# HGRN score steps in smaller pieces, and the sums for a fast matrix product issued in another place and rank

## The chip, the cores and the metric

The kernel runs on one core of a Trainium2 chip. The metric is the device time of one execution in microseconds (us); the median of three runs is 1410.47 us (1410.33 to 1411.88).

## The reference, cut to what matters

One transformer-like block over 256 tokens of width 2048. A normalised input goes through one combined projection; an HGRN2 branch and a chunked attention branch are gated and merged, projected, and followed by a squared-ReLU MLP.

```python
u = rms_norm(h, norm_mix_w)
hq, hf, hi, hg, aq, ak, av, gates = jnp.split(u @ w_in, SPLIT_POINTS, axis=-1)
g = lb + (1.0 - lb) * sigmoid(hf);  log_g = log(g);  kk = 1.0 - g
q = silu(hq) * HG_DK ** -0.5
# per chunk of 64 tokens, 8 heads of 128 channels: b = cumsum(log_g)
scores = einsum('bhtk,bhtsk,bhsk->bhts', qc, exp(b_t - b_s) where t >= s, kc)
o = scores @ v + (decayed state) ...
y_a = rms_norm(o, hg_norm_w) * silu(hg);  y_b = chunk_band_attention(aq, ak, av, rel_bias)
h = h + (gate_a * (y_a @ w_branch_a) + gate_b * (y_b @ w_branch_b)) @ w_out
h = h + square(relu(rms_norm(h, norm_mlp_w) @ w_up)) @ w_down
out = rms_norm(h, norm_final_w)
```

All is float32. w_in has 11,264 columns, w_up and w_down 8192 columns and rows.

## The kernel before, in words

**Matrix products.** Every float32 matrix is split into a high part (a cast on ScalarE, ACT, line 89) and a low part (a subtraction on VectorE, DVE, line 90), and each product is three matmuls on TensorE (PE): high by high, high by low, low by high (lines 143 to 145; 184, 185 and 188 for the transposed form). Weights come in pieces over the SyncE DMA queue into rings of buffers (`raw`, `wh`, `wl`); `split` and the copies and subtractions that TensorE waits for are written inside `tc.high_priority(offset=2000)`.

**Order on the engines.** The kernel is written for a planner: each engine's queue is laid out beforehand, by an operation's rank (its place in the program's text, moved up by 2000 under `high_priority`) among those whose operands and buffers are expected to be ready. On the chip each engine then keeps its queue's order and waits on semaphores. `tc.issue_after(ins)` adds an order edge: what is written in its block stays behind `ins` on the engine of `ins`, with no semaphore.

**HGRN.** The eight heads are done in four pairs (`fq(0)` to `fq(3)`); pairs 0 and 1 make group 0, pairs 2 and 3 group 1. For a pair, `hf_pair` makes the decay g, the keys `kk` and the running sum `b` (a Sigmoid, a logarithm, a scan), `hq_pair` the queries `q` (a Sigmoid). `hgrn_scores` makes the scores of a pair with small matmuls at four levels: `diagonal` (line 372), three `level`s with block sizes 2, 8 and 32 (line 416), and `level128` (line 448). Each level multiplies left factors `kl` by right factors `qr` that `factors` makes on DVE and ACT with exponentials (lines 383 to 405), and merges the product, by mask, from PSUM into `sd` (line 423; `diagonal` at 373 and 374). `hgrn_out` multiplies the scores by `v` (lines 476, 477), normalises and gates into `o` (line 487), and `finish` transposes it (line 494). PSUM for these small products is a ring of two banks (`ps_sm`).

The small steps are spread between the k-tiles of the large projections: `later(...)` appends pairs of a gap in ticks and a step to the list `behind`, and each k-tile of a projection calls `tick`, which counts the gap of the first one down (two ticks for a k-tile in `gemm`, one in `gemm_t`) and runs it at zero. The projections follow in the order hf, hq of pairs 0 and 1, hi of group 0, hg of group 0, hf and hq of pair 2, hf and hq of pair 3, hi and hg of group 1, then the first two of aq.

**Units.** The larger products after that (half of the gates, w_out, w_up, w_down) go through `Unit` and `run`. A unit covers 1024 output columns; for the first half of its rows it uses seven block products instead of eight, which needs sums of weight blocks (`sums` on DVE, `sent` by an accumulating DMA on GpSimd's queue) and sums of blocks of the left operand (`combos`: `one`, `two` and two more `final`s, lines 640 to 657, with a split for each sum into tiles `S`). Partial products go from one PSUM bank to another through `copy` (ACT, line 756) and `less` (DVE, line 783). The second half of the rows is done plainly, in `plain` items of two k-tiles; the last two items of a unit are run within the next unit.

A unit also carries `steps`: transposes of blocks of the next left operand (`one`) and the sums (`combos`). At eleven places of `run`, numbered 0 to 10, `step(at)` runs the first step in the list if `at` has reached the step's own third entry or the unit's `start`. `plain` first runs every step whose first entry is not above its rows' block number (2 or 3): these are forced. The places, in order: ahead of product 12, ahead of product 11 (second), ahead of item (8, 9), ahead of product 21 (first), [first copy `u1`], ahead of item (10, 11), [`less` of 12], ahead of product 21 (second), [second copy `u2`], 6: ahead of item (8, 9) of the other columns, [`less` of 22], 7, 8, 9 and 10 ahead of the remaining item, the last product and the last two items. The steps concerned: `h_blocks(0)` in unit `wo2` (sums of h for w_up), and `turns(0)` in units `up02`, `up12`, `up22` and `up32` (sums of u, the squared-ReLU output, for w_down).

Of the kernel before, what the change touches and what calls it, by code (L numbers as in the profile page):

```python
# [50 lines left out]
def tile_hybrid_block(  # L51
# [107 lines left out]
    def later(*steps):  # L159
        behind.extend([n, f] for n, f in steps)  # L160
# [149 lines left out]
    def hf_pair(u, f):  # L310

        nc.vector.tensor_tensor(f, f, bc(rstd_t, 1, 2), op=ALU.mult)
        nc.scalar.activation(f, f, AF.Sigmoid)
        for h in range(2):
            hh = 2 * u + h
            nc.vector.tensor_scalar(f[:, h, :], f[:, h, :], omlb[:, hh:hh + 1], lb[:, hh:hh + 1],
                                    op0=ALU.mult, op1=ALU.add)
        kk = h2(f"kk{u}")
        nc.vector.tensor_scalar(kk, f, -1.0, 1.0, op0=ALU.mult, op1=ALU.add)
        nc.vector.tensor_scalar(f, f, LN_MIN, None, op0=ALU.max)  # L320
        lg = h2(f"lg{u}")
        nc.scalar.activation(lg, f, AF.Ln)
        b = h2(f"b{u}")
        nc.vector.tensor_tensor_scan(b.rearrange("p h t -> p (h t)"), reset,
                                     lg.rearrange("p h t -> p (h t)"), 0.0, ALU.mult, ALU.add)
        return f, kk, b
# [32 lines left out]
            gws.append(s)  # L359
        return gws  # L360

    def hgrn_scores(n, kk, b, q):
# [92 lines left out]
        def both(*fs):  # L455
            def go():
                for x in fs:
                    x()
            return go

        return (sd, so), [both(diagonal, f[0]), both(l[0], f[1]), both(l[1], f[2]), both(l[2], factors128), level128]

    ya = []

# [46 lines left out]

    def scores(n, a, gap, first=None):
        sc, steps = hgrn_scores(n, *a)
        later(*[(gap if i or first is None else first, f) for i, f in enumerate(steps)])
        return sc

    def group(g, s0, s1, vs, gws, gap, gap2):
        o0, f0 = hgrn_out(g, 0, s0, vs, gws)
        o1, f1 = hgrn_out(g, 2, s1, vs, gws)
        later(*[(gap, f) for f in o0 + o1], *[(gap2, f) for f in f0 + f1])  # L520
# [209 lines left out]
    class Unit:  # L730
# [22 lines left out]

        def copy(self, dst, i):
            with tc.high_priority(offset=2000):
                nc.scalar.copy(dst, self.c[i])
            return dst

        def product(self, i, name, left, first=False):
# [20 lines left out]

        def less(self, i, t):
            with tc.high_priority(offset=2000):
                nc.vector.tensor_tensor(self.c[i], self.c[i], t, op=ALU.subtract)

        def sums(self, dst, src):
            with tc.high_priority(offset=2000):
# [185 lines left out]
    def h_blocks(n0):  # L972

        def one(n, m):
            if not m:
                hT.append(new_act(f"h{n}"))
            hi, lo = hT[n][:, :, 0, :], hT[n][:, :, 1, :]
            t = h1[n][m]
            tp = transpose4(t, f"h{n}{m}")
            tmp = fours(token(f"hw_{n}_{m}"))  # L980
            nc.vector.tensor_tensor(tmp, tp, bc(wmlp[:, 4 * n:4 * n + 4], 2, P), op=ALU.mult)
            split(hi[:, :, m * P:(m + 1) * P], lo[:, :, m * P:(m + 1) * P], tmp)
            nc.scalar.activation(token(f"hsq_{n}_{m}"), t, AF.Square, accum_out=ssq2[:, m, n:n + 1])

        def factor():
            ssum2 = small.tile([P, NM], F32, name="ssum2", tag="ssum")
            nc.vector.tensor_reduce(ssum2, ssq2, axis=AX.X, op=ALU.add)
            rsqrt(rstd2, ssum2, D, NM)

        return [(n, lambda n=n, m=m: one(n, m)) for n in (n0, n0 + 1) for m in range(NM)] + [  # L990
            (n0 + 1, f, 7) for f in ([factor] if n0 else combos(hT, "h", sp, Sh))]

    rstd2 = const.tile([P, NM], F32, name="rstd2")

    def h_out(m, n, acc):
        t = token(f"h1_{n}_{m}")
        with tc.high_priority(offset=2000):
# [7 lines left out]
    rstd3 = const.tile([P, NM], F32, name="rstd3")  # L1005
    NQ = 4
    units = [Unit(lambda: mT, lambda: Sm, w_out, n0 * NC, f"wo{n0}", lambda m, n, acc, n0=n0: h_out(m, n0 + n, acc),
                  steps=(lambda: h_blocks(0)) if n0 else (lambda: turned(mT, 3, "m3", ga)), start=3 if n0 else 0) for n0 in (0, 2)]
    fin = {}
    for qd in range(NQ):  # L1010
        last = qd == NQ - 1
# [2 lines left out]
        def turns(c0, uT=uT, rs=rs, Su=Su, blocks=blocks, qd=qd):  # L1014

            def one(c, m):
                if not m:
                    uT.append(new_act(f"u{qd}{c}"))
                hi, lo = uT[c][:, :, 0, :], uT[c][:, :, 1, :]
                tp = transpose4(rs[c, m], f"u{qd}{c}{m}")  # L1020
                if c < 2:
                    blocks[m, c] = fours(token(f"a{m}{c}_u{qd}"))
                    nc.scalar.copy(blocks[m, c], tp)
                split(hi[:, :, m * P:(m + 1) * P], lo[:, :, m * P:(m + 1) * P], tp)

            return [(c, lambda c=c, m=m: one(c, m)) for c in (c0, c0 + 1) for m in range(NM)] + [
                (c0 + 1, f, 7) for f in ([] if c0 else combos(uT, f"u{qd}", tk, Su, blocks))]

        for c in range(0, 4, 2):
            def done(m, n, acc, c=c, rs=rs, qd=qd):  # L1030
                t = token(f"r{qd}{c}{n}{m}")
                with tc.high_priority(offset=2000):
                    nc.scalar.activation(t, acc, AF.Relu, scale=rstd2[:, m:m + 1])
                nc.scalar.activation(t, t, AF.Square)
                rs[c + n, m] = t

            units.append(Unit(lambda: hT, lambda: Sh, w_up, qd * (FF // NQ) + c * NC, f"up{qd}{c}", done,
                              steps=(lambda turns=turns: turns(0)) if c else (lambda: ()) if qd else (lambda: h_blocks(2)), start=3 if c else 0))

        def out_of(m, n, acc, last=last, qd=qd):  # L1040
            if not last:
# [85 lines left out]
```

## Time and profile before

| | us |
|---|---|
| median of three runs | 1410.47 (1410.33 to 1411.88) |
| the profiled execution | 1411.28 |
| its span, first to last instruction | 1409.5 |
| PE busy | 1387.3 |
| DVE busy | 1119.1 |
| ACT busy | 909.0 |
| GpSimd busy | 137.0 |

In a line of the profile stand the engine, the source line (L416), the tile written and the tiles read. "<-" before an engine and a tile names what ended the idle time in front of an instruction. PEclk is the TensorE clock that was granted, as a share of full speed. A matmul's own duration overlaps with its neighbours'; the distance between starts is what one costs.

### The profile page before, as it was taken

What the parts mean: (1) busy time and instruction counts of PE and PEld (TensorE: products, weight loads), DVE (VectorE), ACT (ScalarE), POOL (GpSimd) and SP (SyncE); (2) the same over time, 40 slices, a digit from 0 to 9 for tenths busy, and PEclk for the clock granted to TensorE, in tenths of its full rate; (3) what the DMA queues carried; (4) which work ended last, traced back from release to release, by engine and by line L of the source; (5) the groups of instructions that cost most, each with busy time, mean ns of one, the idle gap of its engine ahead of it and who ended that gap; (6) DMA issues with size and microseconds to landing.
All of it is one profiled execution on the core that took longest, in us unless ns stands there. A gap on an engine that the chain in (4) does not pass through costs nothing.

```text
span 1409.5 us, 18582 instructions
## 1 busy us (share of the span) xinstructions
PE 1387.3 (98%) x6562; PEld 1149.8 (82%) x6562; DVE 1119.1 (79%) x1410; ACT 909.0 (64%) x1170; POOL 137.0 (10%) x220
## 2 busy tenths in 40 slices
PE   9999999999999999999999999999999999999997
PEld 7878888878787888888778888888888888888885
DVE  7897987675657875687999878789777897878885
ACT  6755745464556665445767876677666876668764
POOL 2000001010000000001210001100111001110200
PEclk9999999999999999999999999999999999999999
DMA  9644445665568987558898898998899888998883
GB/s 336 219 156 156 144 157 162 191 172 167 177 224 262 259 236 257 188 176 254 245 292 263 242 277 225 288 279 249 258 290 292 249 229 252 286 298 261 259 247 118
DMA packets 122925, 327.42 MB, mean 232 GB/s; under 512 B 10944, under 2 KB 11712, under 8 KB 122448
## 3 DMA queue, kind: packets, MB, share of 16 engines
q1 hardware_dynamic: 103264, 264.80, 54.8%
q0 software_dynamic: 18416, 59.84, 21.4%
q10 hardware_dynamic: 1152, 1.60, 0.3%
q8 instruction: 51, 0.84, 0.2%
q14 instruction: 42, 0.34, 0.1%
HBM read 271.67 MB, written 10.49 MB: 200 GB/s over the span
## 4 chain that ended last, share of the span: by engine, by line
PE 93%; DVE 3%; ACT 2%; issue 1%; DMA 0%; POOL 0%; SPq 0%; POOLq 0%; DVEq 0%; ACTq 0%
PE acc_ak L185 2%; PE acc_hq L185 2%; PE acc_aq L185 2%; PE acc_hf L185 2%; PE ps L416 1%; PE tp_u L106 1%; PE acc_ga L144 1%; PE acc_hg L144 1%; PE acc_hg L145 1%; PE acc_hg L143 1%; PE acc_ga L145 1%; PE acc_bb L143 1%; PE acc_ga L143 1%; PE acc_ba L143 1%; PE acc_av L145 1%; PE acc_ba L145 1%
## 5 line engine op out<-in xcount | busy, mean ns | idle before, releaser
L185 PE MATMUL acc_aq<-act_x,wh_aq 128*128 128x512 f32 x128 | 46.6, 401 | 0.0
L185 PE MATMUL acc_hf<-act_x,wh_hf 128*128 128x512 f32 x128 | 45.9, 396 | 0.0
L185 PE MATMUL acc_hq<-act_x,wh_hq 128*128 128x512 f32 x128 | 45.9, 396 | 0.0
L185 PE MATMUL acc_ak<-act_x,wh_ak 128*128 128x512 f32 x128 | 45.2, 398 | 0.0
L90 DVE TENSOR_TENSOR wl_ga<-raw_ga,wh_ga 128x1024 fp32r<-128x1024 f32 x16 | 19.6, 1225 | 19.6 <-ACT wh_ga L89 19.4
L184 PE MATMUL acc_aq<-act_x,wl_aq 128*128 128x256 f32 x120 | 34.9, 291 | 0.0
L184 PE MATMUL acc_hf<-act_x,wl_hf 128*128 128x256 f32 x120 | 34.4, 287 | 0.0
L184 PE MATMUL acc_hq<-act_x,wl_hq 128*128 128x256 f32 x120 | 34.3, 286 | 0.0
L90 DVE TENSOR_TENSOR wl_av<-raw_av,wh_av 128x1024 fp32r<-128x1024 f32 x16 | 19.6, 1224 | 18.1 <-ACT wh_av L89 18.1
L184 PE MATMUL acc_ak<-act_x,wl_ak 128*128 128x256 f32 x120 | 33.8, 281 | 0.0
L89 ACT CAST wh_hg<-raw_hg 128x1024 fp32r<-128x1024 f32 x16 | 16.8, 1050 | 24.2 <-PE acc_hg L145 13.9
L89 ACT CAST wh_bb<-raw_bb 128x1024 fp32r<-128x1024 f32 x16 | 16.9, 1054 | 23.3 <-PE acc_ba L145 17.7
L90 DVE TENSOR_TENSOR wl_bb<-raw_bb,wh_bb 128x1024 fp32r<-128x1024 f32 x16 | 19.6, 1222 | 14.8 <-ACT wh_bb L89 14.8
L89 ACT CAST wh_av<-raw_av 128x1024 fp32r<-128x1024 f32 x16 | 16.8, 1052 | 22.0 <-PE acc_av L145 12.4
L90 DVE TENSOR_TENSOR wl_aq<-raw_aq,wh_aq 128x1024 fp32r<-128x1024 f32 x16 | 19.6, 1223 | 14.2 <-ACT wh_aq L89 14.1
L89 ACT CAST wh_ba<-raw_ba 128x1024 fp32r<-128x1024 f32 x16 | 16.8, 1053 | 20.7 <-PE acc_bb L145 13.8
L89 ACT CAST wh_aq<-raw_aq 128x1024 fp32r<-128x1024 f32 x16 | 16.8, 1048 | 20.0 <-PE acc_hg L145 9.5
L90 DVE TENSOR_TENSOR wl_ba<-raw_ba,wh_ba 128x1024 fp32r<-128x1024 f32 x16 | 19.6, 1223 | 12.4 <-ACT wh_ba L89 12.4
L185 PEld LDWEIGHTS acc_ak<-act_x,wh_ak 128*128 128x128 f32 x128 | 24.0, 188 | 5.6
L185 PEld LDWEIGHTS acc_aq<-act_x,wh_aq 128*128 128x128 f32 x128 | 24.1, 189 | 5.4 <-issue 0.7
L185 PEld LDWEIGHTS acc_hf<-act_x,wh_hf 128*128 128x128 f32 x128 | 24.1, 188 | 5.3 <-DVE f L193 0.3
L185 PEld LDWEIGHTS acc_hq<-act_x,wh_hq 128*128 128x128 f32 x128 | 24.1, 188 | 5.1
(1808 smaller groups left out, 5250.3 us busy)
## 6 DMA issues: line engine op xcount, KB each, us to landing
raw_hi<-in_w_in_n_dram SPq DMA_DIRECT2D x16, 512.0 KB, 4.2
raw_hg<-in_w_in_n_dram SPq DMA_DIRECT2D x16, 512.0 KB, 3.8
raw_aq<-in_w_in_t_dram SPq DMA_DIRECT2D x16, 512.0 KB, 4.0
raw_ak<-in_w_in_t_dram SPq DMA_DIRECT2D x16, 512.0 KB, 3.9
raw_av<-in_w_in_n_dram SPq DMA_DIRECT2D x16, 512.0 KB, 4.4
raw_ga<-in_w_in_t_dram SPq DMA_DIRECT2D x16, 512.0 KB, 4.2
raw_ba<-in_w_branch_a_dram SPq DMA_DIRECT2D x16, 512.0 KB, 4.4
raw_bb<-in_w_branch_b_dram SPq DMA_DIRECT2D x16, 512.0 KB, 4.5
```

The costliest lines, as they stand in the source:

```text
L89: (copy or nc.scalar.copy)(hi, src)
L90: nc.vector.tensor_tensor(lo, src, hi.bitcast(F32), op=ALU.subtract)
L106: nc.tensor.transpose(tp[:, j, :], src[:, j * P:(j + 1) * P], ident)
L143: nc.tensor.matmul(acc, hi, wh, start=first, stop=False, skip_group_check=True)
L144: nc.tensor.matmul(acc, hi, wl, start=False, stop=False, skip_group_check=True)
L145: nc.tensor.matmul(acc, lo, wh, start=False, stop=last, skip_group_check=True)
L184: nc.tensor.matmul(acc[:, cb, 0:T], wl[:, c], r[:, 0, :], start=False, stop=False)
L185: nc.tensor.matmul(acc[:, cb, :], wh[:, c], r.rearrange("p u t -> p (u t)"), start=kt == 0, stop=kt == nkt - 1)
L416: nc.tensor.matmul(ps[:, m, :], klf[:, a * P:(a + 1) * P], qrf[:, a * 192:(a + 1) * 192], start=True, stop=True)
```

## The change

In `hgrn_scores` the five steps (diagonal with factors 2; level 2 with factors 8; level 8 with factors 32; level 32 with the factors of 128; level 128) become eight: diagonal with factors 2, factors 8, level 2, factors 32, level 8, factors 128, level 32, level 128. `hgrn_scores` itself is called when the first of them runs. `fq` no longer makes the decay and the queries; it returns them as two steps. For pairs 0 and 2 they run at once, for pairs 1 and 3 they are put into the list of the pair before. The gaps are set anew, and the scores of pair 2 are queued after the projections of pair 3 instead of ahead of them.

In the units, the sums of h and u and the blocks of `h_blocks(0)` and `turns(0)` get a first entry of 99, so that `plain` no longer forces them; the blocks start at place 0 instead of 3 and the sums at place 6 (one for each place). The sums, and the step `factor` in unit `up00`, are written behind the last `copy` on ACT and the last `less` on DVE with `issue_after`, and with high priority.

```diff
-        return (sd, so), [both(diagonal, f[0]), both(l[0], f[1]), both(l[1], f[2]), both(l[2], factors128), level128]
+        def first():
+            diagonal()
+            f[0]()
+
+        return (sd, so), [first, f[1], l[0], f[2], l[1], factors128, l[2], level128]
...
-        g, kk, b = hf_pair(u, f)
-        return kk, b, hq_pair(u, z, g)
+        made = {}
+        def decay():
+            made["g"], made["kk"], made["b"] = hf_pair(u, f)
+        def query():
+            made["q"] = hq_pair(u, z, made["g"])
+        return made, decay, query
...
+    def scores(n, made, gap, first=None, between=()):
...
+        todo = [(gap if i or first is None else first, lambda i=i: one(i)) for i in range(8)]
+        for at, f in between:
+            todo.insert(at, (gap, f))
+        later(*todo)
...
     a0, a1 = fq(0), fq(1)
-    s0 = scores(0, a0, 8, 20)
+    a0[1]()
+    a0[2]()
+    s0 = scores(0, a0[0], 5, 12, ((5, a1[1]), (8, a1[2])))
     vs0 = v_chunk(0)
-    s1 = scores(1, a1, 8)
+    s1 = scores(1, a1[0], 4)
     gws0 = hg_chunk(0)
+    group(0, s0, s1, vs0, gws0, 5, 4)
     a2 = fq(2)
-    group(0, s0, s1, vs0, gws0, 3, 4)
-    s2 = scores(2, a2, 6)
+    a2[1]()
+    a2[2]()
     a3 = fq(3)
+    s2 = scores(2, a2[0], 4, None, ((2, a3[1]), (5, a3[2])))
     vs1 = v_chunk(1)
-    s3 = scores(3, a3, 6)
+    s3 = scores(3, a3[0], 4)
     gws1 = hg_chunk(1)
-    group(1, s2, s3, vs1, gws1, 2, 3)
+    group(1, s2, s3, vs1, gws1, 3, 3)
...
         def step(self, at):
             if self.steps and at >= (self.steps[0][2] if len(self.steps[0]) > 2 else self.start):
-                self.steps.pop(0)[1]()
+                step = self.steps.pop(0)
+                with ExitStack() as es:
+                    if len(step) > 2:
+                        es.enter_context(tc.issue_after(self.copied.ins))
+                        es.enter_context(tc.issue_after(self.lessened.ins))
+                        es.enter_context(tc.high_priority(offset=2000))
+                    step[1]()
...
-        return [(n, lambda n=n, m=m: one(n, m)) for n in (n0, n0 + 1) for m in range(NM)] + [
-            (n0 + 1, f, 7) for f in ([factor] if n0 else combos(hT, "h", sp, Sh))]
+        return [(n if n0 else 99, lambda n=n, m=m: one(n, m)) for n in (n0, n0 + 1) for m in range(NM)] + [
+            (99, f, 6) for f in ([factor] if n0 else combos(hT, "h", sp, Sh))]
...
-            return [(c, lambda c=c, m=m: one(c, m)) for c in (c0, c0 + 1) for m in range(NM)] + [
-                (c0 + 1, f, 7) for f in ([] if c0 else combos(uT, f"u{qd}", tk, Su, blocks))]
+            return [(c if c0 else 99, lambda c=c, m=m: one(c, m)) for c in (c0, c0 + 1) for m in range(NM)] + [
+                (99, f, 6) for f in ([] if c0 else combos(uT, f"u{qd}", tk, Su, blocks))]
```

`start` of these two kinds of unit goes from 3 to 0; `copy` and `less` keep their instruction in `self.copied` and `self.lessened`; `group` calls `hgrn_out` when its first output step runs.

More of the change, by code (lines that the diff above doesn't have):

```diff
@@ L360, in hg_chunk, with hgrn_scores @@
         return gws
-    def hgrn_scores(n, kk, b, q):
+    def hgrn_scores(n, made):
+        kk, b, q = made["kk"], made["b"], made["q"]
         sd = hp.tile([P, 2, NM, P], F32, name=f"sd{n}", tag="sd", bufs=2)
@@ L755, in copy @@
             with tc.high_priority(offset=2000):
-                nc.scalar.copy(dst, self.c[i])
+                self.copied = nc.scalar.copy(dst, self.c[i])
             return dst
@@ L1007, in tile_hybrid_block @@
     units = [Unit(lambda: mT, lambda: Sm, w_out, n0 * NC, f"wo{n0}", lambda m, n, acc, n0=n0: h_out(m, n0 + n, acc),
-                  steps=(lambda: h_blocks(0)) if n0 else (lambda: turned(mT, 3, "m3", ga)), start=3 if n0 else 0) for n0 in (0, 2)]
+                  steps=(lambda: h_blocks(0)) if n0 else (lambda: turned(mT, 3, "m3", ga)), start=0) for n0 in (0, 2)]
     fin = {}
@@ L1037, in tile_hybrid_block @@
             units.append(Unit(lambda: hT, lambda: Sh, w_up, qd * (FF // NQ) + c * NC, f"up{qd}{c}", done,
-                              steps=(lambda turns=turns: turns(0)) if c else (lambda: ()) if qd else (lambda: h_blocks(2)), start=3 if c else 0))
+                              steps=(lambda turns=turns: turns(0)) if c else (lambda: ()) if qd else (lambda: h_blocks(2)), start=0))
         def out_of(m, n, acc, last=last, qd=qd):
```

28 lines of the change are left out of this document (16 added, 12 removed).

## The prediction

> **What bounds the kernel now.** I read the page first: its shares of busy time and the shares of the chain that ended last.
>
> ```profile
> span 1409.5 us, 18582 instructions
> PE 1387.3 (98%) x6562; PEld 1149.8 (82%) x6562; DVE 1119.1 (79%) x1410; ACT 909.0 (64%) x1170; POOL 137.0 (10%) x220
> PE 93%; DVE 3%; ACT 2%; issue 1%; DMA 0%; POOL 0%; SPq 0%; POOLq 0%; DVEq 0%; ACTq 0%
> ```
>
> TensorE is busy for 1387.3 of 1409.5 us. The change removes no matmul and no transpose, so it can only win back time in which TensorE stands still or runs slowly: 22.2 us of standing, the start and the end of the program included. Next I asked the waits whom TensorE waited for.
>
> ```profile
> PE ps L416 <- DVE qr L405: 2.2, 1, 2.2
> PE acc_wo2c L143 <- ACT u_wo L756: 2.1, 1, 2.1
> PE acc_hf L188 <- DVE wl_hf L90: 1.2, 1, 1.2
> PE ps_warm L81 <- DVE warm L79: 1.1, 1, 1.1
> PE po L477 <- DVE o L487: 1.1, 1, 1.1
> PE acc_ga2c L144 <- DVE wl_ga2p11D L90: 1.0, 1, 1.0
> PE tp_h L106 <- DVE hw L981: 0.8, 1, 0.8
> PE acc_hq L188 <- DVE wl_hq L90: 0.8, 1, 0.8
> PE ps L416 <- DVE sd L374: 0.7, 1, 0.7
> PE acc_wo0c L144 <- DVE wl_wo0r L90: 0.5, 1, 0.5
> PE po L476 <- DVE ms L95: 0.3, 1, 0.3
> ```
>
> These are all of them, 11.8 us, each met once. Four belong to the HGRN part (L416 twice, L477, L476: 2.2 + 0.7 + 1.1 + 0.3 = 4.3 us). Two belong to the unit `wo2`, in which the sums of h are made (2.1 + 0.8 = 2.9 us). Nothing in the four units where the sums of u are made is on the list. The remaining 4.6 us (`ps_warm`, `hf`, `hq`, `ga2`, `wo0`) come before or outside what the diff moves. The third view is the table of windows, for the clock and for the room on VectorE and ScalarE.
>
> ```profile
> core 0: us, PE busy (x) PEld busy (x) DVE busy (x) ACT busy (x) POOL busy (x), PEclk, DMA share, GB/s
> 72.00:76.00 4.00, 1.84 (x10) 1.45 (x9) 4.00 (x9) 3.35 (x7) 0.00 (x0) 0.96 0.29 95
> 76.00:80.00 4.00, 4.00 (x14) 3.25 (x13) 3.08 (x9) 0.73 (x1) 0.00 (x0) 0.62 0.64 227
> 80.00:100.00 20.00, 20.00 (x96) 17.06 (x95) 19.26 (x49) 11.68 (x19) 0.00 (x0) 1.00 0.45 145
> 180.00:200.00 20.00, 20.00 (x97) 17.15 (x96) 19.00 (x46) 11.02 (x18) 0.00 (x0) 1.00 0.49 160
> 200.00:220.00 20.00, 20.00 (x101) 17.29 (x101) 12.17 (x28) 6.58 (x8) 0.00 (x0) 1.00 0.44 142
> 676.00:742.00 66.00, 62.62 (x288) 50.74 (x286) 65.50 (x73) 44.56 (x58) 12.73 (x20) 1.00 0.93 273
> 742.00:800.00 58.00, 58.00 (x265) 47.53 (x264) 51.24 (x55) 46.24 (x64) 4.14 (x5) 1.00 0.88 267
> ```
>
> Behind the longest wait the granted clock falls to 0.62 for 4 us. That loses another 0.38 x 4 = 1.5 us which no list of waits shows, so the wait at L416 really costs 2.2 + 1.5 = 3.7 us. And VectorE is nearly full where the waits lie (65.50 of 66 us around `wo2`), so work that is only moved inside such a stretch still has to be done there.
>
> **The change part by part.** The program's engine queues are planned ahead, by priority and by when operands are expected; an operation may run long before its place in the text, and the trace shows this (the sums of x, written after the attention, run as soon as their memory is free). So "two steps ahead" does not start the factors earlier by itself. What it does is move matmuls to later places than their factors, and rank the next pair's preparation behind them.
>
> *Pair 0's first product.* Its chain, from the timeline:
>
> ```profile
> 62.99 0.48 DVE L338 TENSOR_TENSOR q<-q,f 128x128 f32<-128x128 f32 x2
> 63.80 1.28 ACT L322 ACT_TABLE_LOAD   x1
> 65.10 0.63 ACT L322 ACTIVATE lg<-f 128x512 f32<-128x512 f32 x1
> 65.64 1.46 PE L372 MATMUL ps<-q,kk 128*128 128x192 f32 x8
> 65.75 1.28 ACT L389 ACT_TABLE_LOAD   x1
> 68.54 1.28 ACT L332 ACT_TABLE_LOAD   x1
> 69.83 0.63 ACT L332 ACTIVATE sq<-zq 128x512 f32<-128x512 f32 x1
> 70.48 1.28 ACT L391 ACT_TABLE_LOAD   x1
> 71.71 0.39 PE L143 MATMUL acc_hi<-wh_hi,act_x 128*128 128x512 f32 x1
> 71.94 0.39 PE L144 MATMUL acc_hi<-wl_hi,act_x 128*128 128x512 f32 x1
> 74.28 0.29 DVE L405 TENSOR_TENSOR qr<-qr,rr 128x128 f32<-128x128 f32 x1
> 74.71 1.99 PE L416 MATMUL ps<-qr,kl 128*128 128x192 f32 x8 [2.16 <-DVE qr L405]
> ```
>
> The last factor `qr` ends at 74.57; the product that needs it could have begun 2.16 us earlier. Ahead of it on ScalarE stands pair 1's preparation, which the old text ranks above pair 0's factors: a table load and `lg` (63.80 to 65.73), the load back (1.28), a load and `sq` (68.54 to 70.46) and the load back (1.28), together 1.91 + 1.28 + 1.92 + 1.28 = 6.4 us. The change ranks all of that behind factors 0 to 2 of pair 0, so `qr` can be done up to 6.4 us sooner, near 68. Places: hi's matmuls are issued 0.23 us apart (71.71, 71.94), six to a k-tile, 1.4 us each. The diagonal product moves from 20 ticks to 12 at two ticks per k-tile, four k-tiles earlier: 65.64 - 5.5 = 60.1. The first level comes 3 + 3 k-tiles and the 1.2 us of the diagonal later, at 69.5. So 68 against 69.5: the wait and its clock dip go, **-3.7**.
>
> At its new place the diagonal product needs `q`, which now ends at 63.47. What may replace the old wait is therefore between 0 (the plan sets it later, or `q` comes sooner without pair 1's operations) and 3.4 plus a clock dip of 1.5, 4.9. `q` is first in rank already and the planner fills with hi's matmuls while it expects no `q`, so I take a value near the lower end: **+0.5**.
>
> The Trainium skill, "TensorE: Matmul & The Clock Gate" (Why this matters for your kernels), asks only that gaps of more than about 3 us be avoided, since one idle window puts the array at half clock. By that rule a 2.2 us gap costs 2.2, and this term would be -2.2 instead of -3.7; the clock row above disagrees with it, and the row decides.
>
> *Pair 0 to 3's other products.* Places in the new text, by the same ticks (in the transposed projections a k-tile is one tick, about half as long): levels of pair 0 at 69.5, 79 and 92; pair 1 at about 112, 119, 126; pair 2 from 161 at 171, 180, 187 and pair 3 from 194 to 215, where the old text has pair 2 from 156 at 161, 167, 172 and pair 3 from 186 to 202. VectorE's 19.00 of 20 in 180 to 200 thus spreads into 200 to 220, where it has 12.17. The 0.7 us at L416 (waiting for `sd`, the previous level's merge, which still filled its PSUM buffer) goes when levels stand 7 to 9 us apart instead of 5.4: **-0.7**. Worse than before is bounded by the same row: at most another 0.7 for a pair.
>
> *Output products of group 0.* They wait for `o` and `ms` (1.1 + 0.3 = 1.4), two buffers deep. The old text spaces them 3 ticks (2.1 us) apart with pair 2's factors queued among them; the new one 5 ticks (3.5 us) with pair 2's scores ranked behind pair 3's projections. Pair 2's preparation still stands right ahead of them, so I do not take all of it: **-0.9**, between -1.4 and +0.7 for the tail, where group 1's outputs now come some 10 us later. That tail has cover: the projection of ak can begin only when a projection accumulator is emptied, and aq's second projection runs in between.
>
> *Sums of h, unit `wo2`.* All eight steps (four blocks, four sums) are forced ahead of one product today.
>
> ```profile
> 704.13 1.07 POOL L998 DMA_DIRECT2D h<-in_x_dram  x2 [1.40 <-ACT hsq L983]
> 709.67 0.62 ACT L89 CAST S_h<-a_h 128x512 fp32r<-128x512 f32 x1 [3.82 <-DVE a_h L651]
> 711.14 0.58 ACT L756 COPY u_wo<-acc_wo2c 128x512 f32<-128x512 f32 x1
> 721.99 0.68 DVE L725 TENSOR_TENSOR h<-acc_wo2c,h 128x512 f32<-128x512 f32 x1
> ```
>
> ScalarE stands 3.82 us at the cast of a sum that VectorE has not made, and the copy that TensorE needs is queued behind it: that is the 2.1. The new order edge puts the casts of the sums behind this copy, so the 2.1 goes by construction, and one block per step instead of four at once takes the 0.8. On VectorE the second edge queues the sums behind the subtraction that closes a partial product, which is older work with the same rank; behind the waiting sums stand the splits, whose lead is the price (below). But the stretch is VectorE's: 65.50 of 66 us, so only 0.5 idle, plus what the weights' low parts are ahead of their use at its end:
>
> ```profile
> 737.91 1.22 DVE L90 TENSOR_TENSOR wl_up00p21A<-raw_up00A,wh_up00p21A 128x1024 fp32r<-128x1024 f32 x1
> 740.83 0.39 PE L144 MATMUL acc_up00c<-wl_up00p21A,S_h 128*128 128x512 f32 x1
> ```
>
> Ready at 739.13, used at 740.83: 1.7 us. I credit 0.5 + 1.7 = **-2.2** of the 2.9. If all of the wait survives in another place it is 0; if the order also frees VectorE, -2.9 and the 0.5 at `wo0`, -3.4.
>
> *Sums of u, four units.* No wait stands there, so nothing can be gained beyond noise; the sums move three to seven steps later and now rank among the weights' splits. Cover: 742 to 800 has 6.8 us of idle VectorE. **0**, bounded by 0 (no wait to remove) and +2.1 a unit (the `wo2` wait, once in each). No DMA changes its place in the text. GpSimd's queue, 12.73 of 66 us busy around `wo2`, gets the one power of `factor` a step earlier and, since a sum's four token tiles are held longer, may load rows of x (704.13) later; they are used at 721.99, and I cost both at nothing for those 18 us of cover.
>
> Sum: -3.7 + 0.5 - 0.7 - 0.9 - 2.2 = **-7.0**. The profiled execution took 1411.28 us (its span of 1409.5 and 1.8 around it), 0.8 above the median of 1410.47, so 1404.3 for it and **1403.5** as a median.
>
> **The rivals.** *Waits only move in the HGRN part.* Each of the four preparations now inserted between products (two for pair 1, two for pair 3) brings a load, its function and a load back to ScalarE, 1.28 + 0.63 + 1.28 = 3.2 us, into the middle of a pair. For it: VectorE and ScalarE do the same work in the same stretch. Against it: ScalarE is busy 11.68 of 20 us in 80 to 100, where pair 1's two come. If each costs TensorE 1 us, +4.0: 1407.5. The Trainium skill, "ScalarE: Activation LUTs" (Rules for kernel authors), speaks for this one: do all work of one table set before switching, and it budgets about 2.7 us a switch. Here a load takes 1.28 us and the function follows at once.
>
> *VectorE alone sets `wo2`.* Nothing is gained there: +2.2, 1405.7. For it stands the 65.50; against it, that the sums can wait until after 742.
>
> *Sums in front of splits (slower).* With the splits' rank, a sum's cast stands on ScalarE before its VectorE part is done, as at 709.67, with weight casts behind it instead of the copy; decided when the standstill of 3.8 us is longer than the lead of the splits. At 2.1 in each of five units, 10.5 instead of 2.1, +8.4, and nothing of the 2.2: -4.8 + 8.4 = +3.6, 1414.1. Against it: the low parts of later units are several pieces ahead, and the new place of the sums has fewer blocks around it.
>
> *It does nothing.* Ranks change, but the planned queues come out nearly alike: 1410.5. For it: the old queues already run factors ahead (`el` of the next level before the diagonal); against it: the two largest waits have a named operation ahead of them that is moved.
>
> **How the numbers follow.** Chances: forecast 0.48, HGRN waits move 0.14, VectorE sets `wo2` 0.15, slower 0.14, nothing 0.09. 0.2% is 2.8 us, about what a measurement of this kernel can tell. Faster takes in the forecast, `wo2` and most of the first rival: 0.75; the rest of that one and "nothing" give same 0.11; slower 0.14. The low end takes every bound at its best: -3.7 - 0.7 - 1.4 - 3.4 = -9.2, 1401.3; the largest wait hid 1.5 us of slowed matmuls behind its 2.2, and if the other five (1.1, 0.3, 0.7, 2.1, 0.8) hide half a microsecond for each of theirs, 2.5 more: 1398.8, rounded to 1398.5. The high end is 1411, which leaves out the slower case and little else.
>
> **What would show it.** In the waits of the changed kernel the rows "ps L416 <- qr L405" and "acc_wo2c <- u_wo" are missing and the clock around 76 us is 1.00; a row "ps L372 <- q" would be the new wait; the cast of the first sum of h stands behind the second copy `u_wo`; VectorE stays above 65 of 66 us around `wo2` if the 0.7 I withheld is right. The forecast is wrong if splits of `up` weights (wl_up) show up in the waits, or if several rows of `ps` and `po` replace the four of today.

## The result and the profile after

The changed kernel is slower: a median of 1414.44 us (1412.78 to 1416.57, six runs) against 1410.40 (1407.66 to 1411.88, six runs beside them), a ratio of 1.0032 [1.0018, 1.0046]. The prediction was 1403.5 us, faster. The profiled execution took 1415.05 us, 3.8 more than that of before (1411.28).

The first two lines of the page of after:

```profile
span 1413.2 us, 18595 instructions
PE 1390.6 (98%) x6562; PEld 1153.3 (82%) x6562; DVE 1119.8 (79%) x1410; ACT 908.3 (64%) x1171; POOL 138.4 (10%) x220
```

The work is the same. TensorE is busy for 3.3 us longer with as many matmuls, so some of them ran at a lower clock. The waits of TensorE in after (line, operand, total, times, longest, in us; all of them):

```profile
PE tp_h L106 <- DVE hw L1015: 3.6, 1, 3.6
PE acc_ak L185 <- DVE aq00T L193: 2.4, 1, 2.4
PE acc_hq L188 <- DVE wl_hq L90: 1.7, 1, 1.7
PE acc_up00c L143 <- ACT wh_up00p22A L89: 1.2, 1, 1.2
PE ps_warm L81 <- DVE warm L79: 1.1, 1, 1.1
PE acc_ga2c L144 <- DVE wl_ga2p11D L90: 1.0, 1, 1.0
PE ps L373 <- DVE q L338: 0.5, 1, 0.5
PE acc_hf L188 <- DVE wl_hf L90: 0.5, 1, 0.5
PE acc_up00c L144 <- DVE wl_up00p21A L90: 0.4, 1, 0.4
```

All four HGRN waits of before (`qr`, `sd`, `o`, `ms`, 4.3 us) are gone, and so is the wait for `u_wo` (2.1). But two waits stand here that before did not have or had small: 2.4 us for `aq00T` at the end of the HGRN part, and 3.6 us for `hw` (0.8 before), with two more for weights of `up00`. The table of windows of after shows the clock at three of these places:

```profile
core 0: us, PE busy (x) PEld busy (x) DVE busy (x) ACT busy (x) POOL busy (x), PEclk, DMA share, GB/s
60.00:80.00 20.00, 19.46 (x90) 16.12 (x90) 19.52 (x40) 16.19 (x22) 0.00 (x0) 1.00 0.52 177
240.00:244.00 4.00, 1.65 (x10) 1.03 (x9) 3.63 (x7) 2.72 (x6) 0.43 (x3) 1.00 0.74 219
244.00:248.00 4.00, 4.00 (x17) 3.42 (x16) 3.67 (x8) 0.04 (x1) 0.00 (x0) 0.59 0.36 125
718.00:740.00 22.00, 20.45 (x93) 16.22 (x92) 22.00 (x23) 14.07 (x15) 5.68 (x8) 1.00 0.83 219
744.00:748.00 4.00, 4.00 (x12) 3.38 (x13) 3.00 (x5) 2.31 (x5) 0.00 (x0) 0.50 0.84 271
748.00:752.00 4.00, 4.00 (x16) 3.18 (x15) 1.35 (x2) 1.74 (x4) 0.00 (x0) 0.76 0.92 304
```

The clock fall behind the HGRN product (0.62 in before) is gone: 60 to 80 us runs at 1.00. The two new waits bring falls of their own, to 0.59 and to 0.50.

To see what each part is worth, I divided both traces at the first matmul into the same accumulators. The times below are worked out from these starts, in us; the experiments' columns are explained with them. Differences are taken before rounding, so some are 0.1 off the table.

| stage | before | after | e8 | e12 | e11 | e14 |
|---|---|---|---|---|---|---|
| start, to hi | 53.4 | 55.3 | 53.4 | 53.8 | 53.7 | 53.5 |
| HGRN: hi to ak | 192.0 | 188.2 | 185.6 | 185.6 | 185.6 | 185.6 |
| attention and first gates: ak to `ga2` | 179.7 | 181.0 | 179.6 | 179.4 | 179.3 | 179.6 |
| other gates and branches | 214.3 | 214.3 | 214.4 | 214.4 | 214.4 | 214.3 |
| `wo0` and `wo2` | 83.5 | 79.2 | 83.8 | 79.7 | 81.1 | 81.7 |
| `up00` | 43.1 | 51.4 | 43.1 | 50.6 | 45.7 | 44.1 |
| rest | 633.6 | 633.7 | 633.4 | 633.6 | 635.2 | 633.4 |

Without the start, after is 1.8 us longer than before. The HGRN part wins 3.8 and the attention behind it gives 1.3 back. `wo0` and `wo2` win 4.2, and `up00` gives back 8.3: the three waits of `up00` in the list make 5.2 of these (3.6, 1.2 and 0.4), and the clock of 0.50 and 0.76 in two stretches of 4 us another 3.0. The 1.9 us of the start are a difference between runs: TensorE, VectorE and ScalarE run the same instructions in the same order in both kernels up to about 60 us, and the start took 52.7 to 54.1 in the kernels below. (The last 10 us, behind the last matmul, are alike and left out.)

### The profile page after: what moved, and what is told of

Same layout as the page of the kernel before. It is cut to its first block, busy times and chain, and to the rows that moved or that the text cites. A ratio compares the mean times of both kernels' runs of the same rounds, so it can differ in the third digit from the quotient of the medians.

```text
span 1413.2 us, 18595 instructions
## 1 busy us (share of the span) xinstructions
PE 1390.6 (98%) x6562; PEld 1153.3 (82%) x6562; DVE 1119.8 (79%) x1410; ACT 908.3 (64%) x1171; POOL 138.4 (10%) x220
## 4 chain that ended last, share of the span: by engine, by line
PE 95%; DVE 3%; issue 1%; ACT 1%; DMA 0%; SPq 0%; POOLq 0%; POOL 0%; DVEq 0%; ACTq 0%
PE acc_ak L185 2%; PE acc_aq L185 2%; PE acc_hq L185 2%; PE acc_hf L185 2%; PE ps L417 1%; PE acc_aq L184 1%; PE acc_ga L144 1%; PE acc_ak L184 1%; PE tp_u L106 1%; PE acc_ga L145 1%; PE acc_hg L145 1%; PE acc_hg L144 1%; PE acc_bb L143 1%; PE acc_hg L143 1%; PE acc_av L145 1%; PE acc_bb L144 1%
## 5 line engine op out<-in xcount | busy, mean ns | idle before, releaser
L90 DVE TENSOR_TENSOR wl_ba<-raw_ba,wh_ba 128x1024 fp32r<-128x1024 f32 x16 | 19.6, 1224 | 12.5 <-ACT wh_ba L89 12.5
L89 ACT CAST wh_ak<-raw_ak 128x1024 fp32r<-128x1024 f32 x16 | 16.8, 1051 | 19.7 <-PE acc_ak L185 9.7
```

Of the source, the lines that this page charges most:

```text
L89: (copy or nc.scalar.copy)(hi, src)
L90: nc.vector.tensor_tensor(lo, src, hi.bitcast(F32), op=ALU.subtract)
```

## The experiments

The theory at first: the HGRN part and the units are independent; the HGRN part wins about what was forecast less the `aq00T` wait, and the units lose because the sums rank among the splits. The rivals: the two parts disturb each other; the sums' rank is not the cost but their time, or the blocks of `up00`. Ratios are against the kernel before on the same chip (its medians there: 1409.95 to 1410.77).

### Which part costs what: e1 and e2

e1 has the HGRN lines of the diff and the units of before. e2 has the units of the diff and the HGRN lines of before.

> The HGRN part of the change with the units as they were before. Theory: the trace of the changed kernel has 1.7 us of lost matmul time between 60 and 240 us where the kernel before has 8.7, and 4.3 against 0.2 between 240 and 280, so this part alone is worth -7.0 + 4.1 = -2.9 us: about 1407.5. Rival, the HGRN part is what made the kernel slower: 1412 or more. The waits should show acc_ak <- aq00T (about 2.4 us) and no ps L417 <- qr.

> The units' part of the change with the HGRN part as it was before. Theory: between 680 and 760 us the changed kernel loses 9.0 us where the kernel before loses 4.8, so this part alone costs about +4.2: 1414.6, with the waits tp_h <- hw and splits of up00 in place of acc_wo2c <- u_wo. Rival, the loss comes from both parts together (the units suffer only because the HGRN part moved the planned queues): within 1 us of the kernel before.

e1: 1409.54 us, 0.9991 [0.9982, 1.0001]. e2: 1417.87 us, 1.0056 [1.0044, 1.0069]. The units part alone is the loss (`up00` 52.6 in e2, 43.4 in e1), and the HGRN part alone is worth little. Both times are above what was expected, by 2.0 and 3.3 us. The waits of e1 (first two rows) and of e2 (two rows):

```profile
PE acc_ak L185 <- DVE aq00T L193: 2.3, 1, 2.3
PE acc_wo2c L143 <- ACT u_wo L784: 2.1, 1, 2.1
```

```profile
PE tp_h L106 <- DVE hw L987: 3.5, 1, 3.5
PE ps L416 <- DVE qr L405: 2.2, 1, 2.2
```

Each wait goes with its part, so they don't cause one another. The medians do not add up, though: -0.4 and +7.9 against +4.0 for both. The profiled spans come nearer (-1.8 and +6.7 against +3.7). What makes up the rest stayed open.

### Why ak waits for `aq00T`: e4 and e6

The timeline of after around this wait:

```profile
238.19 0.61 DVE L486 SCALAR_TENSOR_TENSOR o<-po,ro,gw 128x128 f32<-128x128 f32 x2 [0.87 <-POOL ro L96]
241.45 0.58 ACT L192 COPY aq00T<-acc_aq 128x512 f32<-128x512 f32 x1
242.72 0.68 DVE L193 TENSOR_TENSOR aq00T<-acc_aq,aq00T 128x512 f32<-128x512 f32 x1
243.46 0.50 PE L185 MATMUL acc_ak<-act_x,wh_ak 128*128 128x512 f32 x1 [2.35 <-DVE aq00T L193]
```

The copy that empties aq's first accumulator runs only behind the last `o`. aq's tiles lie in a pool opened in the memory of the HGRN tiles, so I took it that the copy waits for that memory. e4 gives the tile `aq00T` a pool that is opened ahead of the HGRN pool (and one token tile fewer, `TOK` 11 to 10, to make room). e6 leaves the tile and moves the outputs up.

```diff
+    aqp = ctx.enter_context(tc.tile_pool(name="aqpool", bufs=1))
     hpool_cm = tc.tile_pool(name="hpool", bufs=1, reuse_waits="tile")
...
+        if what == "aq00":
+            return z_t(col, what, aqp.tile([P, 2, T], F32, name=f"{what}T", tag="aq", bufs=1), factor, acc)
...
-    TOK = 11
+    TOK = 10
```

```diff
-    s3 = scores(3, a3[0], 4)
+    s3 = scores(3, a3[0], 3)
-    group(1, s2, s3, vs1, gws1, 3, 3)
+    group(1, s2, s3, vs1, gws1, 2, 3)
```

> The changed kernel with the tile aq00T in memory of its own instead of memory that the HGRN pool gives free (and one token tile fewer, to make room). Theory, the wait acc_ak <- aq00T is a buffer wait for the last HGRN tile: the copy into aq00T comes right behind the end of its projection, about 230 us instead of 241, the wait is gone and 4.1 us with it: about 1410.5. Rival, the copy is late because ScalarE's queue has the outputs' casts ahead of it: the wait stays and the time is within 1 us of 1414.4.

> The changed kernel with pair 3's score steps 3 ticks apart instead of 4 and group 1's outputs 2 ticks instead of 3: the last outputs come some 5 us sooner. Theory, the wait acc_ak <- aq00T hangs on the end of the last HGRN output: it goes, and with it 3 to 4 us: about 1411. Rival: the outputs then wait for their own chains and the time stays at 1414.

e4: 1411.48 us, 1.0013 [1.0004, 1.0021]. e6: 1411.27 us, 1.0004 [0.9995, 1.0013]. Both lose the wait, and the HGRN stage falls from 188.2 to 185.3 and 185.6, the attention from 181.0 to 179.8 in both. Two rows of the timeline of e4:

```profile
224.33 0.58 ACT L192 COPY aq00T<-acc_aq 128x512 f32<-128x512 f32 x1
236.00 0.61 DVE L487 SCALAR_TENSOR_TENSOR o<-po,ro,gw 128x128 f32<-128x128 f32 x2 [0.87 <-POOL ro L96]
```

The copy now runs 11.7 us ahead of the last `o` rather than behind it. That shows the memory as the cause: the last output is as late as in after (236.0 against 238.2, with a start that was 2.3 us shorter), and ak no longer waits behind it. Of the 4 us that each of the two wins here, `wo0` to `up00` together lose 3.1 again in e4 and 1.6 in e6; no run tells why.

### What won the pair's first product: e5

The prediction gave the gain to the rank of pair 1's preparation (6.4 us of ScalarE behind the factors). e5 is after with both preparations run at once, as before, and the rest of the text kept:

```diff
-    s0 = scores(0, a0[0], 5, 12, ((5, a1[1]), (8, a1[2])))
+    a1[1]()
+    a1[2]()
+    s0 = scores(0, a0[0], 5, 12)
-    s2 = scores(2, a2[0], 4, None, ((2, a3[1]), (5, a3[2])))
+    a3[1]()
+    a3[2]()
+    s2 = scores(2, a2[0], 4)
```

> The changed kernel with the preparation of pairs 1 and 3 made at once, ranked ahead of the scores of pairs 0 and 2 as before the change; the eight steps and their gaps stay. Theory of the prediction, the rank of pair 1's preparation is what delayed the first product of pair 0: its factors end near 74 us again while its place is now near 70, so the wait ps <- qr comes back with 2 us or more and a fall of the clock, 3 to 6 us in all: about 1418 to 1420. Rival, the place of the products (one step more behind their factors) is what won: no such wait, within 1 us of 1414.

The preparations also leave the lists, so the steps that stand behind them there come sooner. It took 1413.33 us, 1.0018 [1.0009, 1.0027], not the 1418 to 1420 that was expected. One row of its waits, the two places in its timeline, and one of its windows:

```profile
PE ps L417 <- DVE qr L406: 1.4, 2, 1.1
```

```profile
71.58 1.21 PE L417 MATMUL ps<-qr,kl 128*128 128x192 f32 x6 [0.33 <-DVE qr L406]
82.67 1.54 PE L417 MATMUL ps<-qr,kl 128*128 128x192 f32 x8 [1.11 <-DVE qr L406]
```

```profile
60.00:80.00 20.00, 19.18 (x88) 15.72 (x87) 18.84 (x40) 17.34 (x24) 0.00 (x0) 1.00 0.42 138
```

The wait for `qr` comes back in two pieces, without the clock fall (1.00 from 80 to 88 us too), and the larger piece is at the second level, not at the first product. Counted from the first matmul of `hi`, the last `qr` of the first product ends at 21.2 us in before, 17.4 in e5 and 15.9 in after; the product starts at 21.3, 17.5 and 17.1. So the rank of the preparation makes 1.5 of the 5.3 us by which `qr` comes sooner. The product itself is not later than before. Over the whole stage the rank is worth about 2 us (187.7 against 185.6 in e6; neither waits for `aq00T`). The other 4.3 of the 6.4 us between before and e6 come with what e5 keeps: the earlier diagonal product, the smaller steps and their gaps. No run separates these.

### The HGRN part with a closer tail: e8

e8 is e1 with the two gaps of e6.

> The HGRN part alone, units as before, with the closer gaps at the tail (pair 3 at 3 ticks, outputs at 2). Theory: the HGRN part alone was 1409.5 with 2.3 us and a fall of the clock lost at acc_ak <- aq00T; without these about 1406, faster than both kernels. Rival, the tail's loss moves into the outputs: 1409.5 as before.

1405.12 us (1403.21 to 1407.18), 0.9957 [0.9945, 0.9970]: faster than both kernels. The HGRN stage is 6.4 us shorter than before and the units are as before. Of the four waits 0.3 us is left, and the new one at the diagonal product is the 0.5 of after. All kernels below but e3, e7 and e9 have this HGRN part.

### Why `up00` loses: rank, time or place of the sums (e3, e12, e11)

The chain that ended last, in order of time, from where `up00` stands still in after (start, us, what):

```profile
737.45 0.90 DVE wl_up00p21A L90
738.35 0.23 issue
738.59 1.22 DVE wl_up00r L90
739.81 0.37 DVE wl_up00p21B L90
740.17 0.68 issue
740.86 1.22 DVE wl_up00p21B L90
742.08 1.14 DVE wl_up00r L90
743.22 0.61 DVE hw L1015
743.96 1.30 PE tp_h L106 x5
745.26 0.43 PE acc_up00c L143
745.69 0.43 PE acc_up00c L144
```

From 711 to 743 us the chain of after runs from one VectorE instruction to the next; TensorE does not stand on it. `hw` is a block of h that TensorE has transposed and VectorE scales; until VectorE has read it, its PSUM bank, one of two, is not free for the next block. The first two blocks of `up00` were transposed by 731.7 us, but `hw` comes after two splits `wl_up00p21B` (739.72 to 742.08) and one `wl_up00r`. The low parts `wl_up00p21B` are first used at 753.38, 11.3 us later, but splits carry the high rank and `hw` does not. Behind the wait matmuls are 0.43 us apart instead of 0.23.

Three experiments vary the sums of h. e3 is after without their high priority:

```diff
-                        es.enter_context(tc.high_priority(offset=2000))
                     step[1]()
```

e12 is e8 with the sums as in after (not forced, place 6, behind the copy, high priority), and the blocks as before. e11 is e8 with the blocks as in after (not forced, one for each place from 0), and the sums forced ahead of one item, (10, 11), at low rank and without order edges.

> The changed kernel without the one line that gives the sums the splits' rank; the sums stay unforced, at place 6, behind the copy and the subtraction. Theory, the rank is the cost: VectorE makes the splits of the next unit first, the leads of the low parts after 715 us stay above 1 us, the 3.6 us wait tp_h <- hw shrinks or goes, and of the 9.0 us lost between 680 and 760 less than 5 remain: about 1410. Rival, VectorE's work sets this stretch whatever the order: 9 us are lost as before and the time stays at 1414.

> The HGRN part with the closer tail (1405.1); of the units' part only the sums (unforced, place 6 on, behind copy and subtraction, with the splits' rank); the blocks forced together as before. Theory, late sums fill VectorE when up00 begins: up00 loses 5 us or more, wo2 under 2: 1408 to 1411. Rival, sums behind the copy are the gain: the 2.1 us wait for u_wo goes and nothing comes back, 1403.

> The HGRN part with the closer tail (1405.1); of the units' part only the blocks, from place 0 on, one for each place; the sums stay forced and of low rank, now at item (10, 11), with no edge. Theory, the lateness of the sums is the cost and the spreading of the blocks is the gain: the wait tp_h <- hw of wo2 goes, up00 loses under 2 us: 1404 to 1405. Rival, the spreading itself costs: 1408 or more with waits in up00.

| | us | ratio | `wo0`+`wo2` | `up00` |
|---|---|---|---|---|
| e3 | 1413.63 | 1.0024 [1.0014, 1.0033] | 79.4 | 50.2 |
| e12 | 1411.29 | 1.0011 [1.0003, 1.0020] | 79.7 | 50.6 |
| e11 | 1404.72 | 0.9964 [0.9952, 0.9976] | 81.1 | 45.7 |

The theory that the rank alone is the cost fell with e3: without it `up00` still takes 50.2. But e3 does not clear the rank either. Its low parts of the sums come 20 to 25 us later than in after, counted from the first matmul of `wo2`, and TensorE waits elsewhere: 2.3 us for `wl_wo2r` and 1.9 for the sums `S_h` themselves. The sums' part of the change (e12) reproduces the loss against e8, 7.5 us in `up00`, and the same wait in the timeline of e12:

```profile
739.18 1.23 PE L106 MATMUL tp_h<-ident,h 128*128 128x128 f32 x5 [3.56 <-DVE hw L1015]
```

The blocks spread one by one (e11) do not: they win 2.7 in `wo2` and lose 2.6 in `up00`, nothing in sum. So the cost lies in what was done to the sums. In `wo2` they no longer stand ahead of the product's copy, which goes with the 4.2 us that `wo0` and `wo2` win. What happens to them on VectorE shows in the row of their low parts, in before and in after:

```profile
L90 DVE TENSOR_TENSOR S_h<-a_h,S_h x4: 682/683/691, 710.3 to 737.3; 128x512 fp32r<-128x512 f32 x4
```

```profile
L90 DVE TENSOR_TENSOR S_h<-a_h,S_h x4: 682/684/694, 711.5 to 717.4; 128x512 fp32r<-128x512 f32 x4
```

Before makes three of the four from 736 to 738 us, behind the splits `wl_up00p11A` to `wl_up00p11D`. After makes all four by 718, ahead of nearly all of these. Counted from the first matmul of `wo2`, the splits `wl_up00p22A` to `wl_up00p11D` end 1.4 to 2.4 us later than in before, and TensorE, 4.2 us ahead, asks for them sooner. VectorE cannot make this good: it is busy for 22.00 of 22 us from 718 to 740, as it was before (21.81). Which of the three edits to the sums (no longer forced, order edges, rank) costs how much stays open; forced sums with the high rank were not run. This is after's VectorE in the stretch where it happens, from the timeline:

```profile
705.55 2.49 DVE L668 TENSOR_TENSOR a_h<-act_h 128x512 f32<-128x512 f32 x4
710.86 0.61 ACT L89 CAST S_h<-a_h 128x512 fp32r<-128x512 f32 x1
716.80 1.28 DVE L90 TENSOR_TENSOR S_h<-a_h,S_h 128x512 fp32r<-128x512 f32 x2
```

From the four block additions to the last low part of a sum is 12.5 us. In the same stretch the matmuls of `wo2` use up the lead of the splits: by the ends of the splits and the first matmuls that read them, 5.8 us at 711 us and 0.1 to 0.9 from 719 to 739, for the splits used next. In before it is 1.7 to 6.9 from 719 to 743.

### Whose turn it is on VectorE: e7, e10

e7 is after with the blocks of `up00` at the rank of the splits. e10 is e8's HGRN part with e7's units.

```diff
+        def ranked(n, m):
+            with ExitStack() as es:
+                if n0:
+                    es.enter_context(tc.high_priority(offset=2000))
+                one(n, m)
...
-        return [(n if n0 else 99, lambda n=n, m=m: one(n, m)) for n in (n0, n0 + 1) for m in range(NM)] + [
+        return [(n if n0 else 99, lambda n=n, m=m: ranked(n, m)) for n in (n0, n0 + 1) for m in range(NM)] + [
```

> The changed kernel with the four block steps of h in unit up00 given the splits' rank as well. Theory, the 3.6 us wait tp_h <- hw is an inversion: VectorE makes splits 9 to 12 us ahead of their use while the block that TensorE needs stands behind them by rank; with the rank the wait and the fall of the clock behind it go, of the 8.8 us lost in up00 less than 4 remain: about 1408 to 1410. Rival, VectorE has no time left in this stretch: the wait turns into waits for splits of the same sum and the time stays within 1.5 us of 1414.

> HGRN part with the closer tail (1405.1 with the units as before), and the units' part of the change with the ranked blocks of h. Theory: these units lose 5.8 us in wo2 and up00 where the units before lose 5.1 to 5.4, so about 1405.5 and no gain over the old units. Rival, without the HGRN tail's delay the units' part is a gain: 1403 or less.

e7: 1410.09 us, 1.0000 [0.9991, 1.0008]. e10: 1406.56 us, 0.9976 [0.9967, 0.9986]. In e7 `up00` falls from 51.4 to 47.1. The wait for `hw` is gone from its waits, and smaller ones stand in its place:

```profile
PE tp_h L106 <- DVE h L753: 2.2, 1, 2.2
PE acc_up00c L144 <- DVE wl_up00r L90: 0.7, 2, 0.4
```

No clock fall follows the 2.2 us. So the order of `hw` behind the splits is worth about 4 of the 8.3 us. The rest stays in this order too, and e10 is not ahead of e8, which keeps the old units.

### Less work on VectorE: e9, e13, e14, e15

e9 is after with the four block additions of h on GpSimd. e13, e14 and e15 make the same edit on e10, e8 and e11.

```diff
-            nc.vector.tensor_tensor(a[m, j], x[:, :, 0, :], x[:, :, 1, :], op=ALU.add)
+            (nc.gpsimd if what == "h" else nc.vector).tensor_tensor(a[m, j], x[:, :, 0, :], x[:, :, 1, :], op=ALU.add)
```

> The changed kernel with the four additions that make blocks of h (2.7 us of VectorE) done by GpSimd. Theory, VectorE's time sets the stretch from w_out's second unit to the first w_up unit: 2.7 us less of it there save about that much, 9.2 us lost in the two units become 6 to 7, and the time about 1411.5. Rival, only the rank of h's blocks in up00 matters (the 3.6 us wait): it stays, and so does the time, 1414.

> The closer HGRN tail, the units' part of the change with ranked blocks (1406.6), and the four additions of h on GpSimd. Theory, VectorE's time is what the late sums lack: the 4.5 us lost in wo2 and up00 fall to 2 or less and the time to 1403 to 1404.5. Rival, with the blocks ranked the inversion is gone and VectorE has enough: no change, 1406.5.

> The closer HGRN tail with the units as before (1405.1), and the four additions of h on GpSimd. Theory, VectorE's time: the forced sums are then ready sooner too, the casts ahead of the copy u_wo wait less, the 2.1 us wait shrinks: 1403. Rival, the order of ScalarE's queue holds the copy whatever VectorE has to do, and GpSimd's additions, 2.3 to 3.9 us each instead of 0.7, are later than VectorE's: the wait grows, 1406 or more.

> The closer HGRN tail, the blocks spread with the sums forced at item (10, 11) (1404.7), and the four additions of h on GpSimd. Theory, VectorE's time: the 3.1 us lost in up00 fall under 1.5: 1402.5 to 1404. Rival, the sums wait longer for GpSimd: 1405 or more.

| | us | ratio | the same with VectorE |
|---|---|---|---|
| e9 | 1407.40 | 0.9984 [0.9974, 0.9993] | after, 1.0032 [1.0018, 1.0046] |
| e13 | 1404.33 | 0.9951 [0.9937, 0.9964] | e10, 0.9976 [0.9967, 0.9986] |
| e14 | 1404.04 (1403.18 to 1404.13) | 0.9951 [0.9939, 0.9963] | e8, 0.9957 [0.9945, 0.9970] |
| e15 | 1405.64 | 0.9959 [0.9946, 0.9973] | e11, 0.9964 [0.9952, 0.9976] |

The row of the additions among the instructions of the tile `a_h`, in after and in e9 (durations in ns, least, median and most; first and last start in us):

```profile
L668 DVE TENSOR_TENSOR a_h<-act_h x4: 684/685/686, 705.6 to 707.4; 128x512 f32<-128x512 f32 x4
```

```profile
L668 POOL TENSOR_TENSOR a_h<-act_h x4: 2267/2865/3899, 691.9 to 703.4; 128x512 f32<-128x512 f32 x4
```

In e9 the loss in `up00` falls from 8.3 to 2.7 us, and the time by about 4 us more than was expected. 2.5 us leave VectorE, and the additions also begin up to 14 us earlier (11 counted from the first matmul of `wo2`), since the order edges hold only ACT and DVE; e9 does not tell these two apart. The wait for `hw` is 0.9 us in it. With the old units (e14) what is gained lies within the intervals: the wait for `u_wo` is 1.4 instead of 2.1, and the clock fall that follows it in e8 (0.57 from 704 to 708 us) is gone. With the spread blocks (e15) nothing is gained: the forced sums wait for GpSimd, and the row that e11 had got down to 0.3 is back among the waits:

```profile
PE acc_wo2c L143 <- ACT u_wo L784: 2.4, 2, 2.1
```

e14 has the lowest median, 1404.04 us; e13, e8 and e11 are level with it within their intervals. All four beat both kernels.

## Why the prediction was wrong

In the profiled executions, the HGRN steps were forecast at -4.8 us and came to -2.5 with the attention behind them; `wo2` was forecast at -2.2 and came to +4.1 with `up00`. Another 1.9 is the start, which the change does not touch.

**Pair 0's first product (-3.7): right in size, half right in its reason.** The row "ps L416 <- qr" is missing and the clock from 60 to 80 us is 1.00. `qr` was put near 68 and the product at 69.5; they came at 71.2 and 72.4, with a start 1.9 us later. But the reason named was 6.4 us of preparation that ranks behind the factors, and e5 gives that rank 1.5 of the 5.3 us by which `qr` is sooner. The rest came with the new steps, gaps and places, and in that respect the size was luck.

**The new wait at the diagonal (+0.5): right.** The timeline of after:

```profile
63.71 0.59 PE L373 MATMUL ps<-q,kk 128*128 128x192 f32 x2 [0.54 <-DVE q L338]
```

The product came at 63.7 where the ticks gave 60.1, or 62.0 with the later start, and waited 0.54 us there. That the planner set it near `q` fits this and is not shown.

**The other HGRN waits (-0.7 and -0.9): right, and a little more.** With the tail closed (e8) the HGRN stage wins 6.4 us net where these steps and the two above add up to 4.8.

**The tail of group 1: the first step that failed.** The text said "That tail has cover: the projection of ak can begin only when a projection accumulator is emptied, and aq's second projection runs in between." The sentence names what then waited. The accumulator is emptied into a tile whose memory the last HGRN tiles hold, so later outputs hold up that copy as well; aq's second projection does lie in between and was too short. It cost 2.35 us and, at 0.59 of the clock for 4 us, 1.6 more: 4.0 against the bound of +0.7. The stages agree: e6 wins 2.6 in HGRN and 1.2 in the attention.

**Sums of h in `wo2` (-2.2): the second step that failed.** The wait there did go, and `wo0` and `wo2` won 4.2 us, more than was credited and more than the bound of 3.4. What failed is the lead of 1.7 us that was counted as a gain, and the bounds behind it: "If all of the wait survives in another place it is 0". VectorE had 0.5 us idle in 66; with `wo2` shorter, `up00` needed its low parts sooner than VectorE could make them, and a delayed `hw` cost a wait of 3.58 us with a clock fall behind it. The lead was not room but the cover of the next unit, and using it up cost more than the wait removed: +8.3 in `up00`, +4.1 net for a step bounded by 0. Of the signs named for this step, one held and one did not: the first cast of a sum (710.86) does stand behind the second copy `u_wo` (704.64), but VectorE did not stay above 65 of 66 us from 676 to 742. It was busy for 64.58, and all of its idle time, 1.42 us, lies before 718: the sums left a gap on it early and then there was none until 740.

**Sums of u (0): right.** The rest of the kernel took 633.7 us against 633.6. The slower rival's number (1414.1) came close to the result, but not as it was told: it priced 2.1 us at casts on ScalarE in each of five units, and the loss is in one unit, on VectorE. What it had right is that the sums come to stand in front of splits. The rival that VectorE alone sets `wo2` had the engine right and the unit wrong: `wo2` won, and `up00` paid. The sign that the prediction named for being wrong came: a split of `up` weights, `wl_up00p21A`, stands in the waits with 0.4 us, beside a high part, `wh_up00p22A`, with 1.2. Both stand below `hw`, which stood behind such splits.

**Left open.** The median of after is 4.0 us above that of before; the stages of the one profiled execution, without the start, are only 1.8 longer. A wait for `wl_dn30r` of 0.3 to 1.6 us comes and goes in the last stage (633.4 to 635.8) with no edit near it. No run tells the causes of either.

## What to carry to other kernels

Where one engine is full for a long stretch, find the next instructions that TensorE needs of it behind the stretch, and price a moved piece of work by their lead, not by the wait that it leaves: the lead is spent once and then every microsecond shows, and a fall of the clock can come on top. In a queue ordered by rank, look whether something that TensorE needs now stands behind prefetched work that it needs 10 us later. And when work on an old tile is delayed, ask which later tile takes its memory, and who waits for that one.

## What the runs showed of the hardware

The granted clock can fall after gaps of little more than 2 us. Gaps of 2.16 us (before, `qr`) and 2.35 us (after, `aq00T`) were each followed by 4 us at 0.62 and 0.59; one of 3.58 us by 0.50 and 0.76 in two stretches of 4 us. But a gap of this length does not always bring a fall. The wait of 2.05 us for `u_wo` in before lies in this window, at 1.00:

```profile
700.00:720.00 20.00, 17.95 (x79) 14.55 (x78) 19.84 (x25) 13.72 (x19) 2.16 (x4) 1.00 0.90 325
```

The same wait in e8, 2.06 us, was followed by 0.57 from 704 to 708 us, while 2.21 us in e7 (`h`, at 719) and 2.26 in e3 (`wl_wo2r`, at 726) were followed by 1.00. So these runs give no threshold, and none shows what decides. It also means that the low end of the prediction, which counted a slowed clock behind the other waits, had no row for it. Gaps of 1.1 us did not show a fall (e5, at 82.67 us: 1.00 from 80 to 88). The Trainium skill, "TensorE: Matmul & The Clock Gate" (Why this matters for your kernels), asks that gaps of more than about 3 us be avoided; these rows say that a gap of a little over 2 us can be enough.

An addition of 128x512 float32 took 0.68 us on VectorE and 2.27 to 3.90 on GpSimd, 3.3 to 5.7 times as long, beside a busy VectorE; the profile's spans on GpSimd are rough. The Trainium skill, "GPSIMD Engine Reference" (3.1 Elementwise — side-by-side cycle accounting), measures 1.96 times for a float32 addition with N=2048. What the difference comes from, no run here shows. In the changed kernel the edit paid all the same (1.0032 to 0.9984); with the sums of before it was worth no more than the intervals (e14 against e8).
